# Where an attention stage turns its keys and queries: other slots, and the evictions shared out anew

## The chip, the cores and the metric

The kernel runs on one core of one Trainium2 chip. The metric is the device time of one execution in microseconds; of a kernel with several runs the median is given. The profile is that of one execution.

## The reference, cut to what matters

The program is a two-layer encoder trunk over 1024 tokens of width 1024, in float32. Layer 0 mixes RWKV-7 and gated DeltaNet heads; layer 1 is softmax attention over chunks of 64 tokens, each against its own and the previous 8 chunks. Every layer then has an MLP and a gated embedding. The change lies in layer 1:

```python
def chunk_band_attention(h, w_qkv, q_g, k_g, rel_bias):
    qkv = (h @ w_qkv).reshape(bsz, seq, 3, C_HEADS, C_HEAD_DIM)
    q = rmsnorm(qkv[:, :, 0], q_g) * (C_HEAD_DIM ** -0.5)
    k = rmsnorm(qkv[:, :, 1], k_g)
    v = qkv[:, :, 2]
    ...
    s = jnp.einsum('bqhd,bkhd->bhqk', q_c, k_b).astype(jnp.float32) + bias
    s = jnp.where(valid, s, -jnp.inf)
    prob = jax.nn.softmax(s, -1).astype(v.dtype)
    return jnp.einsum('bhqk,bkhd->bqhd', prob, v_b)
```

and in what is begun beside it: the embedding's projection `rmsnorm(p[i] @ ple_w_proj[i], ple_norm_g[i])` and the output projection of the attention.

## The kernel before, in words

Every float32 operand of a matrix product is kept as a high part (rounded to the matmul's fp32r) and a low part (what the rounding left). ScalarE makes the high part, VectorE the low part by subtraction, and a product is three matmuls (high x high, high x low, low x high).

`attention` runs 73 steps, `k` from -8 to 64. The heads go in pairs; a pair has two tiles of 512 tokens, so there are 16 tiles `s`, each with four steps (two heads `h`, two blocks of 256 queries `blk`): step `k` belongs to tile `k // 4`. All of it is written in program order and kept so: `Pinned` (L105) wraps VectorE, ScalarE and GpSimd, and `mm` and `tr` do the same for TensorE. Each engine works through its list in order, so an instruction that waits holds up all behind it on its engine.

A step is woven from these pieces, with `fill()` between them, which gives TensorE the next three matmuls of the projections (`dense`, eight times in a step):

- `evict(k+7)`: a projected block goes from its bank (`dps`) to `qk` and `vs` (two ScalarE activations, one VectorE subtraction). In some steps a weight is loaded (L1906) and split (`wq`).
- `values(k-1)` (probabilities times values, to `po`) and, every second step, `outs` (`otmp` on ScalarE, `y` on VectorE).
- first slot: `scores(k+1, 0)`, `turn(k, 0)`, `exps(k+1, 0)`, `low(k, 0)`.
- second slot: `scores(k+1, 1)`, `turn(k, 1)`, `turn(k, 2)`, `exps(k+1, 1)`, `low(k, 1)`, `low(k, 2)`.

`scores` writes the only scores buffer (`sc`, two PSUM banks). VectorE reads it at once in one instruction that adds the bias and takes the row's minimum (`pb,mx<-sc,toep`, a second small instruction fetches `mx`). The next `scores` can't begin before that. `exps` is the exponential on ScalarE, `turn` transposes 128 x 128 blocks of probabilities on TensorE into a bank `pt` and copies the high part out (`ptile`), `low` makes the low part on VectorE. `pt` banks come from a pool of three, taken in turn (`bank`, L1980). A step needs two or three of them, by the number of key blocks. Steps of an even tile's second block need two, of an odd tile's three.

Before the scores of tile `s`, its queries and keys must be normalised and turned:

- `squares` (GpSimd) and `sums` (VectorE) in steps 4s-5 and 4s-4, then `norms(s)` in step 4s-4: 14 small GpSimd instructions on 16 columns (`ss`, `nn`, `rsw`) and two products of 512 columns (`qk<-qk,nn`), keys first.
- `heads(s, 1)` at the end of step 4s-3 (`k % 4 == 1`): four transposes of the keys into a bank, then the evictions to `F1`, `k` of the tile. Per head one ScalarE activation (high part, 64 x 512, scaled by `kg`) and one VectorE operation (low part into the other half of the partitions).
- `heads(s, 0)` in step 4s-2, after `outs` and ahead of that step's first scores: four transposes of the queries, per head a ScalarE activation to `F0` and a VectorE operation to `Ql`, alternating, then two more ScalarE activations that write the high part a second time, into the other half of the partitions.

The projections' stream (`filler`, L2249 of before) goes on after the last `dense` with the embedding's projection `ple`. `ple` squares its blocks on ScalarE, adds them up on GpSimd (`act<-act,sq`, L2198) and ends with `row_stats`: sixteen column sums on TensorE (`dps<-ones,act`) and a small chain on VectorE (L282 to L287, L375) for `prsc`, which is next read in the second half of the MLP. After it comes `out_first`, the output projection of the first half of the tokens, which waits for the attention's outputs.

Of the kernel before, what the change touches and what calls it, by code (L numbers as in the profile page):

```python
# [8 lines left out]
F32 = mybir.dt.float32  # L9
F32R = mybir.dt.float32r  # L10
I32 = mybir.dt.int32
AF = mybir.ActivationFunctionType
ALU = mybir.AluOpType
# [102 lines left out]
class Trunk:  # L116
# [1775 lines left out]
    def attention(self, l1):  # L1892


        nc, tc, a, psm, sm, wp = self.nc, self.tc, self.a, self.psm, self.sm, self.wp
        V, A, G = (Pinned(tc, e) for e in (nc.vector, nc.scalar, nc.gpsimd))
        self.pinned, self.done = True, {}
        W, raws, toeps, dps, ST, JOB = {0: self.wq}, {}, {}, {}, {}, {}
        halves = (slice(0, 64), slice(64, 128))
# [62 lines left out]
        def norms(s):  # L1962
            st = ST[s]
            ss = st["ss"]
            nn = sm.tile([P, 16], F32, tag="nn1", name="nn1")
            w = sm.tile([P, 16], F32, tag="rswq", name="rsw")
            G.tensor_scalar(ss, ss, 1.0 / 64, 1e-6, op0=ALU.mult, op1=ALU.add)
            G.tensor_scalar(nn.bitcast(I32), ss.bitcast(I32), -0.5, 1597463007.0, op0=ALU.mult, op1=ALU.add)
            for _ in range(3):
                G.tensor_tensor(w, nn, nn, op=ALU.mult)  # L1970
                G.tensor_tensor(w, w, ss, op=ALU.mult)
                G.tensor_scalar(w, w, -0.5, 1.5, op0=ALU.mult, op1=ALU.add)
                G.tensor_tensor(nn, nn, w, op=ALU.mult)
            q5 = st["qk"].rearrange("p i (j h d) -> p i j h d", j=2, h=2)
            n4 = nn.rearrange("p (i j h) -> p i j h", i=4, j=2)
            for j in (1, 0):
                n = n4[:, :, j, :].rearrange("p i (h o) -> p i h o", o=1).broadcast_to((P, 4, 2, 64))
                G.tensor_tensor(q5[:, :, j], q5[:, :, j], n, op=ALU.mult)

        def bank():  # L1980
            return psm.tile([P, HB], F32, tag="pt", name="pt", bufs=3)

        def heads(s, j):
            st, qk = ST[s], ST[s]["qk"]
            g = self.vec("kg") if j else self.dv["qg8"]
            pt = bank()
            for e in range(4):
                self.tr(pt[:, e * P:(e + 1) * P], qk[:, e, j * P:(j + 1) * P], self.ident)
            if j:
                F = st["k"] = l1.tile([P, 2, HB], F32R, tag="F1", name="F1", bufs=3)  # L1990
            else:
                F = st["Q"] = self.xp.tile([P, 2, HB], F32R, tag=f"x{6 + s % 2}", name="F0")
                lo = st["Ql"] = self.ql[s % 2]
                if s < 2:
                    for h in range(2):
                        G.memset(lo[h][64 * (1 - h):64 * (2 - h)].bitcast(F32), 0.0)
            for h in range(2):
                r, o = halves[h], halves[1 - h]
                A.activation(F[r, h], pt[r], AF.Copy, scale=g[r])
                V.scalar_tensor_tensor(F[o, h] if j else lo[h][r], pt[r], g[r], F[r, h].bitcast(F32),  # L2000
                                       op0=ALU.mult, op1=ALU.subtract)
            if not j:
                for h in range(2):
                    r, o = halves[h], halves[1 - h]
                    A.activation(F[o, h], pt[r], AF.Copy, scale=g[r])

        def job(k):
            if k in JOB:
# [66 lines left out]
        def low(k, b):  # L2075
            jb = JOB[k]
            if b < len(jb["used"]):
                t, pt, u = jb["pts"][b]
                V.tensor_tensor(t[:, 1, u], pt[:, u], t[:, 0, u].bitcast(F32), op=ALU.subtract)
# [43 lines left out]
        E = {}  # L2123
# [45 lines left out]
        def y_split(q, hf):  # L2169
            t, raw = self.act([P, 2, 2, HB], F32R), yraw.pop((q, hf))  # L2170
            for e in range(2):
                ys[2 * q + e, hf] = t[:, e]
                if (q, e, hf) == (3, 1, 1):
                    self.ylast = t[:, e]
                else:
                    self.split_scaled(t[:, e], raw[:, e], None, slice(0, HB))

        def ple():
            act = self.act
            acc = act([P, 2, HB], F32, "b")  # L2180
            t = [act([P, 2, 2, HB], F32) for _ in range(4)]
            self.pnd = [self.dr.tile([P, 2, HB], F32, tag=f"pnd{k}", name="pnd") for k in range(NK)]
            self.prsc = self.cst.tile([P, NT], F32, tag="prsc", name="prsc")
            for n in range(NK):
                if n % 4 == 0:
                    hi, lo = late(n // 4)
                for hf in range(2):
                    ps = self.bank()
                    hs = slice(hf * HB, hf * HB + HB)
                    for k in range(2):  # L2190
                        o = slice(256 * (n % 4) + P * k, 256 * (n % 4) + P * k + P)
                        self.mm3(ps, hi[:, o], lo[:, o], E["w"][k][:, 0, hs], E["w"][k][:, 1, hs], k == 0, k == 1)
                        yield 0
                    nc.vector.tensor_scalar(t[n // 2][:, n % 2, hf, :], ps, self.dv["hpleg"][:, 8 + n:9 + n], None, op0=ALU.mult)
                    sq = acc[:, hf, :] if n == 0 else wp.tile([P, HB], F32, tag="sq", name="sq", bufs=1)
                    nc.scalar.activation(sq, ps, AF.Square)
                    if n:
                        nc.gpsimd.tensor_tensor(acc[:, hf, :], acc[:, hf, :], sq, op=ALU.add)  # L2198
                nc.sync.dma_start(out=self.pnd[n], in_=t[n // 2][:, n % 2])
            self.row_stats([acc[:, 0, :], acc[:, 1, :]], self.prsc)  # L2200

        def out_first():
            self.xh = [self.dr.tile([P, HB], F32, tag=f"xh{k}", name="xh") for k in range(NK)]
            self.order, self.wod = list(range(8)), {}
            yield ("ys", 0)
            y, x4 = {k: ys[k, 0] for k in range(8)}, None
            for n in range(NK):
                w = late(2 + n)
                if n > 1:
                    self.wod[n] = self.dr.tile([P, 2, T], F32, tag=f"wod{n}", name="wod")  # L2210
                    for e in range(2):
                        nc.sync.dma_start(out=self.wod[n][:, e], in_=w[e].bitcast(F32))
                if n % 4 == 0:
                    x4 = self.act([P, 4, HB], F32)
                x = x4[:, n % 4, :]
                nc.sync.dma_start(out=x, in_=self.xd[n][:, 0:HB])

                def ev(ps):
                    nc.vector.tensor_tensor(x, x, ps, op=ALU.add)
                    nc.sync.dma_start(out=self.xh[n], in_=x)  # L2220
                if n == 4:
                    y_load(0, 1)
                if n == 5:
                    y_split(0, 1)
                    y_load(1, 1)
                if n == 6:
                    y_split(1, 1)
                    y_load(2, 1)
                yield from self.dense_part(w, y, ev, self.order)
            y_split(2, 1)  # L2230
            y_load(3, 1)
            ws = [late(10), late(11)]
            self.first = [self.bank() for _ in ws]

            def part(ks):
                for (hi, lo), ps in zip(ws, self.first):
                    for k in ks:
                        o = slice(k * P, k * P + P)
                        self.mm3(ps, hi[:, o], lo[:, o], ys[k, 1][:, 0, :], ys[k, 1][:, 1, :], k == 0, k == 7)
                        yield 0  # L2240
            yield from part(range(6))
            y_split(3, 1)
            self.done["ylast", 0] = 0
            yield from part([6])
            yield ("at", 15)
            yield from part([7])
            self.y = {k: ys[k, 1] for k in range(8)}
# [19 lines left out]
        has = lambda k: 0 <= k < 64  # L2267
        for k in range(-8, 65):
# [37 lines left out]
            if has(k - 1) and k % 2 == 0:  # L2306
                outs(k - 1)
                if k % 4 == 0:
                    finish(k // 4 - 1)
            if k % 4 == 2 and has(k + 2):  # L2310
                heads((k + 2) // 4, 0)
            if has(k + 5) and k % 4 == 3:
                squares((k + 5) // 4, 0)
            if has(k + 4) and k % 4 == 0:
# [8 lines left out]
            fill()  # L2323
            if has(k):
                low(k, 0)
            if has(k + 1):
                scores(k + 1, 1)
            if has(k + 5) and k % 4 == 3:
                sums((k + 5) // 4, 0)
            if has(k + 4) and k % 4 == 0:  # L2330
# [11 lines left out]
                low(k, 1)  # L2342
                low(k, 2)
            if k % 4 == 1 and has(k + 3):
                heads((k + 3) // 4, 1)
            fill()
            if k == -8:
                ps = bank()
# [101 lines left out]
```

## Time and profile before

| | us |
|---|---|
| median of 3 runs | 3072.59 (3068.97 to 3077.63) |
| the profiled execution | 3075.75 |
| its span | 3074.0 |
| TensorE busy (share of the span) | 2947.6 (96%) |
| mean granted TensorE clock | 0.976 of full speed |
| attention stage, from the first `evict` to the last `values` | about 1686 to 2265 |

A row of the timeline gives start, duration, engine, source line, operation, output<-inputs, shape and count, and in brackets how long the engine had stood idle before and what ended that. Two instructions of one kind that follow each other are merged into one row. A row of the waits gives the total, the number of times and the longest. A row of the windows gives the stretch, its length, the busy time and count of PE, PEld, DVE, ACT and POOL, the granted clock, the DMA share and GB/s. PE is TensorE, PEld its weight load, DVE VectorE, ACT ScalarE, POOL GpSimd. L113 is the line of the wrapper, so names of tiles tell such rows apart: `F` is `F0` or `F1`.

### The profile page before, as it was taken

How to read it: one execution, taken by the hardware profiler on the slowest of the kernel's cores; microseconds unless marked ns; L12 is line 12 of the kernel's file. 1: busy time of each engine (PE TensorE's matmuls, PEld its weight loads, DVE VectorE, ACT ScalarE, POOL GpSimd, SP SyncE). 2: the span in 40 equal slices, each digit the busy share in tenths (PEclk: the TensorE clock that was granted, in tenths of full speed). 3: DMA queues.
4: the chain of work that ended last, by engine and by line, in shares of the span. 5: the costliest groups of instructions: out<-in, count | busy, mean ns of one | idle time of the engine just before them, and what ended most of it. 6: DMA issues, size and time to landing. Idle time of an engine off the chain costs nothing. (4 is left out here: it accounts for less than half of the span.)

```text
span 3074.0 us, 45073 instructions
## 1 busy us (share of the span) xinstructions
PE 2947.6 (96%) x16792; PEld 2472.8 (80%) x16792; DVE 2112.4 (69%) x3248; ACT 1412.6 (46%) x2546; POOL 1355.1 (44%) x1668
## 2 busy tenths in 40 slices
PE   8999999999989999999999999999899999999999
PEld 6888778887777888788887888888687888788887
DVE  6756765667758788877676456566647888877672
ACT  4444443444435444543333465566635444543331
POOL 5535533445504766554534322222403666645442
PEclk9999989999999999999999999999999999999999
DMA  3231212212544433754324111111355444654322
GB/s 129 95 96 56 76 42 77 75 59 88 174 169 155 156 149 151 263 182 157 124 89 136 43 38 47 40 40 59 129 203 189 154 151 151 223 209 177 124 96 101
DMA packets 166764, 374.30 MB, mean 122 GB/s; under 512 B 41360, under 2 KB 45584, under 8 KB 165136
## 3 DMA queue, kind: packets, MB, share of 16 engines
q1 hardware_dynamic: 134288, 312.68, 29.5%
q10 hardware_dynamic: 32256, 58.73, 5.0%
q8 instruction: 132, 2.16, 0.3%
q14 instruction: 88, 0.72, 0.1%
HBM read 259.15 MB, written 112.20 MB: 121 GB/s over the span
## 5 line engine op out<-in xcount | busy, mean ns | idle before, releaser
L173 PE MATMUL dps<-r,act 128*128 128x512 f32 x4440 | 1045.2, 394 | 13.1 <-DVE act L113 8.5
L173 PEld LDWEIGHTS dps<-r,act 128*128 128x128 f32 x4440 | 836.5, 189 | 204.6 <-DVE act L113 15.2
L173 PE MATMUL dps<-xg,whi 128*128 128x512 f32 x1248 | 419.7, 414 | 14.1 <-ACT xg L343 6.9
L113 ACT CAST act<-late 128x512 fp32r<-128x512 f32 (+1 forms) x282 | 205.5, 731 | 442.9 <-DVE late L113 258.1
L113 DVE TENSOR_TENSOR act<-late,act 128x512 fp32r<-128x512 f32 (+1 forms) x282 | 330.0, 1172 | 71.5 <-ACT act L113 68.2
L173 PE MATMUL dps<-wq,act 128*128 128x384 f32 x1536 | 340.9, 353 | 1.1 <-ACT gw L1738 0.9
L173 PEld LDWEIGHTS dps<-xg,whi 128*128 128x128 f32 x1248 | 236.3, 195 | 64.8 <-ACT xg L343 6.8
L173 PEld LDWEIGHTS dps<-wq,act 128*128 128x128 f32 x1536 | 264.4, 193 | 4.8 <-ACT gw L1738 1.3
L173 PE MATMUL dps<-xg,wlo 128*128 128x512 f32 x624 | 256.3, 411 | 0.0
L113 POOL TENSOR_TENSOR late<-late 128x512 f32<-128x512 f32 (+1 forms) x104 | 187.8, 1813 | 81.4 <-ACT late L113 58.4
L113 POOL TENSOR_TENSOR late<-late,rs 128x512 f32<-128x512 f32 x88 | 137.5, 1575 | 101.5 <-DVE late L113 94.0
L113 DVE TENSOR_TENSOR r<-act,r 128x1024 fp32r<-128x1024 f32 (+1 forms) x80 | 139.2, 1741 | 6.7 <-ACT r L113 6.7
L113 DVE TENSOR_TENSOR late<-late 128x512 f32<-128x512 f32 x120 | 142.3, 1186 | 1.0
L173 PEld LDWEIGHTS dps<-xg,wlo 128*128 128x128 f32 x624 | 121.2, 194 | 25.7 <-DVE wlo L300 0.4
L173 PE MATMUL dps<-xw,act 128*128 128x512 f32 x576 | 137.8, 392 | 0.0
L113 ACT CAST ptile<-pt 128x512 fp32r<-128x512 f32 (+1 forms) x144 | 74.0, 515 | 134.7 <-PE pt L178 134.3
L113 DVE TENSOR_TENSOR ptile<-pt,ptile 128x512 fp32r<-128x512 f32 (+1 forms) x144 | 83.9, 600 | 68.2 <-ACT ptile L113 67.2
L173 PEld LDWEIGHTS dps<-xw,act 128*128 128x128 f32 x576 | 108.4, 188 | 24.2
L300 DVE TENSOR_TENSOR wlo<-wraw,whi 128x1024 fp32r<-128x1024 f32 x76 | 95.1, 1253 | 39.2 <-ACT whi L299 38.3
L299 ACT CAST whi<-wraw 128x1024 fp32r<-128x1024 f32 x76 | 79.6, 1048 | 89.2 <-PE dps L173 45.9
L113 DVE TENSOR_TENSOR late<-late,dps 128x512 f32<-128x512 f32 x154 | 104.6, 682 | 19.7 <-ACT late L113 15.9
L113 ACT ACTIVATE late<-late 128x512 f32<-128x512 f32 x176 | 110.6, 631 | 13.5 <-POOL late L113 9.8
(509 smaller groups left out, 5711.2 us busy)
## 6 DMA issues: line engine op xcount, KB each, us to landing
late<-in_w SPq DMA_DIRECT2D x100, 512.0 KB
hc<-late ACTq DMA_DIRECT2D x154, 256.0 KB
act<-hc SPq DMA_DIRECT2D x76, 512.0 KB
wraw<-in_w_in SPq DMA_DIRECT2D x56, 512.0 KB
hraw<-hc SPq DMA_DIRECT2D x36, 512.0 KB
hc<-sums ACTq DMA_DIRECT2D x70, 256.0 KB
act<-in_w SPq DMA_DIRECT2D x28, 512.0 KB
wraw<-in_w_out SPq DMA_DIRECT2D x21, 512.0 KB
```

The costliest lines, as they stand in the source:

```text
L113: return lambda *args, **kw: self.tc.keep_in_program_order(f(*args, **kw))
L173: r = self.nc.tensor.matmul(out, lhsT, rhs, start=start, stop=stop)
L299: nc.scalar.copy(hi, raw)
L300: nc.vector.tensor_tensor(lo, raw, hi.bitcast(F32), op=ALU.subtract)
```

## The change

It has five parts. (1) `heads` no longer alternates: both ScalarE high parts come first, then both VectorE low parts, the latter in a function that is returned and called later. (2) For queries, the second copy of the high part is made by GpSimd from the first, where ScalarE read it from the bank again. (3) Keys are turned in the second slot of step 4s-3: the transposes and high parts ahead of that slot's scores, the low parts behind them. Queries are turned at the end of the same step, half a step earlier than before. (4) `norms` runs on VectorE for tile 0, where nothing else is there to be done yet. (5) `ple` no longer ends with `row_stats`; it is called after the second block of `out_first`.

```diff
@@ norms
+            G = V if s == 0 else Pinned(tc, nc.gpsimd)
@@ heads
             for h in range(2):
                 r, o = halves[h], halves[1 - h]
                 A.activation(F[r, h], pt[r], AF.Copy, scale=g[r])
-                V.scalar_tensor_tensor(F[o, h] if j else lo[h][r], pt[r], g[r], F[r, h].bitcast(F32),
-                                       op0=ALU.mult, op1=ALU.subtract)
-            if not j:
+
+            def low():
                 for h in range(2):
                     r, o = halves[h], halves[1 - h]
-                    A.activation(F[o, h], pt[r], AF.Copy, scale=g[r])
+                    V.scalar_tensor_tensor(F[o, h] if j else lo[h][r], pt[r], g[r], F[r, h].bitcast(F32),
+                                           op0=ALU.mult, op1=ALU.subtract)
+                if not j:
+                    for h in range(2):
+                        G.tensor_copy(F[halves[1 - h], h], F[halves[h], h])
+            return low
@@ ple
-            self.row_stats([acc[:, 0, :], acc[:, 1, :]], self.prsc)
+            E["acc"] = [acc[:, 0, :], acc[:, 1, :]]
@@ out_first
                 yield from self.dense_part(w, y, ev, self.order)
+                if n == 1:
+                    self.row_stats(E["acc"], self.prsc)
@@ attention, the steps
-            if k % 4 == 2 and has(k + 2):
-                heads((k + 2) // 4, 0)
...
+            key = k % 4 == 1 and has(k + 3) and heads((k + 3) // 4, 1)
             if has(k + 1):
                 scores(k + 1, 1)
+            if key:
+                key()
...
             if k % 4 == 1 and has(k + 3):
-                heads((k + 3) // 4, 1)
+                heads((k + 3) // 4, 0)()
```

On TensorE, in the step that turns the keys of tile 4 (`pt<-ident,qk` are the transposes of keys or queries, `pt<-ident,pb` those of probabilities, `sc` the scores, `dps<-wq` the projection), this stood before, from the second slot's last scores to the step's end:

```order
L173 MATMUL sc<-F_16667,Ql 128x256
L173 MATMUL dps<-wq_16041,act 128x384
L173 MATMUL dps<-wq_16042,act 128x384
L173 MATMUL dps<-wq_16041,act 128x384
L178 MATMUL pt<-ident,pb 128x128 x4
L173 MATMUL dps<-wq_16041,act 128x384
L173 MATMUL dps<-wq_16042,act 128x384
L173 MATMUL dps<-wq_16041,act 128x384
L178 MATMUL pt<-ident,pb 128x128 x2
L178 MATMUL pt<-ident,qk 128x128 x4
```

The changed kernel has, from just before that slot's scores:

```order
L178 MATMUL pt<-ident,qk 128x128 x4
L173 MATMUL sc<-F_16283,F_16677 128x384
L173 MATMUL sc<-F_16283,Ql 128x384
L173 MATMUL sc<-F_16647,F_16677 128x256
L173 MATMUL sc<-F_16647,Ql 128x256
L173 MATMUL dps<-wq_16041,act 128x384
L173 MATMUL dps<-wq_16042,act 128x384
L173 MATMUL dps<-wq_16041,act 128x384
```

and, behind these, to the step's end:

```order
L178 MATMUL pt<-ident,pb 128x128 x4
L173 MATMUL dps<-wq_16041,act 128x384
L173 MATMUL dps<-wq_16042,act 128x384
L173 MATMUL dps<-wq_16041,act 128x384
L178 MATMUL pt<-ident,pb 128x128 x2
L178 MATMUL pt<-ident,qk 128x128 x4
```

The first `qk` row is now the keys, ahead of the scores; the last, where the keys stood, is the queries.

On VectorE, at the same place, this stood before, from the second slot's reading of the scores (`ISA pb,mx<-sc,toep`) to the first one of the next step (`F` low parts of the keys, `Ql` those of the queries):

```order
L113 ISA pb,mx<-sc,toep 128x640
L113 ISA mx 128x1
L113 TENSOR_TENSOR ptile<-pt,ptile 128x512
L113 TENSOR_TENSOR ptile<-pt,ptile 128x256
L113 SCALAR_TENSOR_TENSOR F_17028<-pt,vecs,F_17028 64x512 x2
L113 SCALAR_TENSOR_TENSOR vs<-dps,rscol,vs 128x128
L113 TENSOR_TENSOR y<-po,otmp 64x512
L113 SCALAR_TENSOR_TENSOR Ql<-pt,d_qg_85,F_17070 64x512 x2
L113 ISA pb,mx<-sc,toep 128x640
```

and this stands there now:

```order
L113 ISA pb,mx<-sc,toep 128x640
L113 ISA mx 128x1
L113 SCALAR_TENSOR_TENSOR F_16999<-pt,vecs,F_16999 64x512 x2
L113 TENSOR_TENSOR ptile<-pt,ptile 128x512
L113 TENSOR_TENSOR ptile<-pt,ptile 128x256
L113 SCALAR_TENSOR_TENSOR Ql<-pt,d_qg_85,F_17038 64x512 x2
L113 SCALAR_TENSOR_TENSOR vs<-dps,rscol,vs 128x128
L113 TENSOR_TENSOR y<-po,otmp 64x512
L113 ISA pb,mx<-sc,toep 128x640
```

The keys' low parts moved ahead of the probabilities' low parts, the queries' ahead of `vs` and `y`.

## The prediction

> **What bounds the kernel now.** I read the shares of the engines first, then TensorE's own waits inside the attention stage (1690 to 2265 us), then the timeline of single steps. TensorE has by far the most to do:
>
> ```profile
> PE 2947.6 (96%) x16792; PEld 2472.8 (80%) x16792; DVE 2112.4 (69%) x3248; ACT 1412.6 (46%) x2546; POOL 1355.1 (44%) x1668
> ```
>
> So a stall of TensorE is time, and what another engine gains is none unless TensorE waited for it. In the attention stage its two largest waits are these (total, times, longest):
>
> ```profile
> PE sc L173 <- DVE mx L113: 43.0, 25, 3.5
> PE dps L173 <- POOL act L2198: 4.2, 1, 4.2
> ```
>
> The first row is a scores matmul that waits until VectorE has read the one scores buffer (`mx` ends that reading). The timeline shows where. Here is a step pair after which a tile with an odd number is turned (tile 3); its step has two probability banks, and I call it short:
>
> ```profile
> 1796.97 0.28 PE L173 MATMUL sc<-F,F 128*128 128x256 f32 x1
> ...
> 1797.37 2.06 POOL L113 TENSOR_TENSOR qk<-qk,nn 128x512 f32<-128x512 f32 x2
> ...
> 1798.32 0.48 ACT L113 CAST ptile<-pt 128x384 fp32r<-128x384 f32 x1 [0.65 <-PE pt L178]
> 1798.59 0.60 PE L178 MATMUL pt<-ident,qk 128*128 128x128 f32 x4
> 1798.71 0.51 ACT L113 ACTIVATE pb<-pb,mx 128x256 f32<-128x256 f32 x1
> ...
> 1802.23 0.35 DVE L113 SCALAR_TENSOR_TENSOR vs<-dps,rscol,vs 128x128 fp32r<-128x128 f32 x1
> 1802.44 0.42 PE L173 MATMUL sc<-F,F 128*128 128x384 f32 x1
> ...
> 1802.80 0.68 DVE L113 TENSOR_TENSOR y<-po,otmp 64x512 f32<-64x512 f32 x1 [0.22 <-ACT otmp L113]
> ...
> 1804.29 0.68 ACT L113 ACTIVATE F<-pt,d_qg 64x512 fp32r<-64x512 f32 x1 [0.81 <-DVE Ql L113]
> 1805.01 0.76 DVE L113 SCALAR_TENSOR_TENSOR Ql<-pt,d_qg,F 64x512 fp32r<-64x512 f32 x1 [0.75 <-ACT F L113]
> 1805.79 0.56 DVE L113 CUSTOM_DVE_ANT_0 pb<-sc,toep 128x384 f32<-128x384 f32 x1
> ...
> 1806.42 0.50 PE L173 MATMUL sc<-F,F 128*128 128x512 f32 x1 [2.01 <-DVE mx L113]
> ```
>
> The scores of 1802.44 are not read until 1805.79, because the query evictions (Ql, in a chain ACT, DVE, ACT, DVE) stand in front of that reading. TensorE stops 2.01 us. Even tiles (three banks, long) lose 2.19, and the last three tiles 3.04, 2.20 and 3.46:
>
> ```profile
> 1828.69 2.06 POOL L113 TENSOR_TENSOR qk<-qk,nn 128x512 f32<-128x512 f32 x2
> ...
> 1829.35 0.34 PE L173 MATMUL sc<-F,F 128*128 128x384 f32 x1
> ...
> 1831.65 0.60 PE L178 MATMUL pt<-ident,qk 128*128 128x128 f32 x4
> ...
> 1832.00 1.81 PE L173 MATMUL dps<-wq,act 128*128 128x384 f32 x9
> ...
> 1840.44 0.47 PE L173 MATMUL sc<-F,F 128*128 128x128 f32 x1 [2.19 <-DVE mx L113]
> ...
> 2132.74 0.50 PE L173 MATMUL sc<-F,F 128*128 128x512 f32 x1 [3.04 <-DVE mx L113]
> 2167.78 0.37 PE L173 MATMUL sc<-F,F 128*128 128x128 f32 x1 [2.20 <-DVE mx L113]
> ...
> 2211.49 0.50 PE L173 MATMUL sc<-F,F 128*128 128x512 f32 x1 [3.46 <-DVE mx L113]
> ```
>
> **The change, part by part.**
>
> *Queries at the step's end.* They leave the place in front of the reading, 15 times: tiles 1 to 12 at 6 x 2.01 + 6 x 2.19 = 25.2, with the last three 33.9 us. What is late next there? In a short step I follow the two queues from the new order. ScalarE: the key's two high parts, the cast of 0.48, the exponential of 0.51 with its sum (0.70 together), the query's two high parts. The evictions last:
>
> ```profile
> L113 ACT ACTIVATE F<-pt,vecs x32: 668/682/686, 1709.3 to 2205.0; 64x512 fp32r<-64x512 f32 x32
> L113 DVE SCALAR_TENSOR_TENSOR Ql<-pt,d_qg,F x32: 733/750/758, 1712.8 to 2210.1; 64x512 fp32r<-64x512 f32 x32
> ```
>
> With the key transposes ending at 1799.08 (below) that gives 1800.55, 1801.05, 1801.6 and 1803.0; VectorE adds two query low parts of 0.75 (1804.55), vs 0.35 and y 0.68, and starts the reading at 1805.6, done after 0.6 at 1806.2. TensorE, later by the key wait, wants the buffer at 1805.9. A stall of 0.3 stays, 7 x 0.3 = 2.1. In a long step the same walk ends the reading at 1839.2, TensorE comes at 1839.7: none.
>
> *Keys in the second slot.* The transposes now stand ahead of the slot's scores, so at 1796.97 and 1829.35, and must wait for GpSimd's multiplication of the keys (the first half of the qk rows): 1797.37 + 1.05 = 1798.42 and 1828.69 + 1.05 = 1829.74. That is a new stall of 1.5 in the 7 short steps, 10.5 us, and 0.45 in six of the 7 long ones, 2.7 (at tile 14 the keys were ready in time). GpSimd's chain begins a step earlier, behind VectorE's sums, where the change moves nothing, so it ends when it did. For tile 15 GpSimd is later still:
>
> ```profile
> 2196.74 0.31 PE L173 MATMUL sc<-F,F 128*128 128x256 f32 x1
> ...
> 2200.00 2.07 POOL L113 TENSOR_TENSOR qk<-qk,nn 128x512 f32<-128x512 f32 x2
> ...
> 2201.12 0.66 PE L178 MATMUL pt<-ident,qk 128*128 128x128 f32 x4 [1.44 <-POOL qk L113]
> ```
>
> 4.3 us in place of the 1.44 there and about 0.5 between: 2.4 more. Behind the waiting transposes everything of TensorE is queued, for it runs in order.
>
> *The banks.* Three banks `pt` go round. In a long step the new order fills all three before the queries, whose transposes need the key's bank. Its last reader is VectorE's second key low part: transposes end 1829.80 + 0.60 = 1830.40, two high parts end 1831.88, two low parts 1833.45. TensorE comes to the query transposes at 1831.65 + 0.45 + 0.35 (one set of four, 1831.65 to 1832.00) = 1832.45 and waits 1.0: 7 x 1.0 = 7 us. In short steps the bank is free.
>
> *GpSimd's copies* replace two ScalarE evictions. Nearest rows for their price:
>
> ```profile
> L113 POOL COPY rl<-l x16: 609/610/1098, 1748.1 to 2257.5; 128x512 f32<-128x512 f32 x16
> ```
>
> ```profile
> 1826.71 1.23 DVE L113 TENSOR_TENSOR wq<-wraw,wq 128x1024 fp32r<-128x1024 f32 x1 [0.58 <-ACT wq L113]
> ...
> 1826.93 1.09 POOL L113 TENSOR_TENSOR rsw<-rsw,ss 128x16 f32<-128x16 f32 x1
> ```
>
> 0.6 to 1.1 each, so ready some 2 us after the query's high parts; the first scores that need them come a step and a half, some 12 us, later: nothing, for that step covers them. Were it gone, the scores would wait up to 2.2. The last two rows show a GpSimd operation on 16 columns that takes as long as VectorE's weight split beside it. [...] In these steps no weight split stands behind the copies, so I take 0 for VectorE too.
>
> *Tile 0.* VectorE takes over its normalisation, and tile 0's queries go too:
>
> ```profile
> 1701.53 0.69 DVE L113 TENSOR_REDUCE ss<-sq 128x8 f32<-128x512 f32 x1 [0.77 <-POOL sq L113]
> ...
> 1708.59 0.66 PE L178 MATMUL pt<-ident,qk 128*128 128x128 f32 x4 [1.17 <-POOL qk L113]
> ...
> 1719.69 0.39 PE L173 MATMUL sc<-F,F 128*128 128x256 f32 x1 [2.32 <-DVE mx L113]
> ```
>
> ```profile
> L285 DVE TENSOR_TENSOR rsw<-prsc 128x8 f32<-128x8 f32 x3 | 0.5, 167 | 0.1
> ```
>
> The last row is VectorE's nearest to the fourteen small operations; with a little between them I take 0.2 each. From 1702.2 they end at 1705, and a product of 0.7 (y above) to 1.05 (GpSimd's) gives keys at about 1706, when the transposes are due: 1.1 gained. The 2.32 falls to about half (the scores' reading still waits for a weight split): 1.1. Together 2.2; between 0 and 3.5.
>
> *Row sums.* They move behind two blocks of the output projection:
>
> ```profile
> 2229.30 3.84 PE L173 MATMUL dps<-ones,act 128*128 128x1 f32 x16 [4.23 <-POOL act L2198]
> ...
> 2234.75 1.05 ACT L2153 CAST wq<-wraw 128x1024 fp32r<-128x1024 f32 x1 [4.88 <-DMA wraw<-in_w_out]
> ```
>
> The 4.23 goes, for the sums of GpSimd are long done by then; but the second row is next on that path, and its weights land when they land. I take 4.2, between 0 and 6.
>
> *The clock.* After some of the stalls TensorE ran at half clock (the granted clock is the third number from the end):
>
> ```profile
> 1840.00:1844.00 4.00, 3.56 (x13) 3.27 (x14) 1.81 (x5) 2.49 (x6) 0.00 (x0) 0.57 0.00 0
> 2132.00:2136.00 4.00, 3.26 (x12) 3.19 (x13) 2.43 (x6) 3.46 (x6) 0.00 (x0) 0.73 0.07 20
> 2168.00:2172.00 4.00, 4.00 (x17) 3.68 (x17) 1.58 (x4) 2.37 (x5) 0.00 (x0) 0.58 0.00 0
> ```
>
> The first and the last lose (1 - 0.575) x 4 = 1.7 us each; I take that for all three. They follow the stalls of 2.19, 3.04 and 2.20. The new stalls are at most 1.5 (but for tile 15), so I let all three go: 5.1 us, between 0 and 5.1. [...]
>
> *Sum*: -33.9 + 2.1 + 10.5 + 2.7 + 2.4 + 7.0 = -9.2; -2.2, -4.2, -5.1: **-20.7 us**. The profiled execution took 3075.75 (span 3074.0 and 1.75 around it), which gives 3055.0; it lies 3.2 above the median of 3072.6, so I predict 3072.6 - 20.7 = **3052**.
>
> **Rivals.**
> A, *only the attention counts*: the clock stays as it is, the row sums' 4.2 returns as the wait for weights, and the short steps keep 0.8, not 0.3: -9.2 - 2.2 + 3.5 = -7.9, 3065. For it: the wait of 4.88; against it: the clock's rows. 0.18.
> B, *slower*: the queries' evictions reach VectorE so late that the reading of the scores still waits for them. It has 1.7 us of room in the short step (1804.55 against some 1806.2); ScalarE's queue there is full from 1799.2 on, and one more wait of that size decides. Then the old stalls stay and the new ones come on top: +15.6 + 7.0 - 2.2 - 4.2 = +16, 3089. Against it: the evictions no longer alternate (0.81 and 0.75 of idling fall away). 0.09.
> C, *the copies hold VectorE up*: as GpSimd's 1.09 waits out VectorE's split, VectorE could wait out two copies of 0.6 in all 15 tiles, 15 x 1.2 = 18, leaving -3, 3070. Against it: the rows show it only the one way round. 0.03. [...]
> The forecast has 0.70.
>
> **How the numbers follow.** A change within 0.3% (9.2 us) can't be told from none. Faster by more: the forecast and a little of A, 0.72; A and C mostly inside, 0.19; slower 0.09. The range: without bank wait and short-step remainder (9 us) and with 2 us more at the row sums 3041; with rival C and without part of the tail 3072. B is left out.
>
> **What would show it.** Right: the 2.01 and 2.19 behind `mx` are gone, TensorE waits for `qk` of GpSimd some 1.5 us at odd tiles, 0.45 at even ones, 4 at the last; the query transposes wait about 1 for VectorE at even tiles; no 4.23 at the row sums; half clock only in the last tiles. Wrong: stalls of 2 us behind `mx` in these steps (B), key waits well over 1.5, or a scores row that waits for GpSimd's copies.

## The result, and the profile after

The changed kernel took 3051.94 us (median of 4 runs) beside 3070.78 us before; the ratio is 0.9932 (0.9909 to 0.9955). The prediction was 3052 from 3072.6. A second set of runs gave 3058.57 us beside 3076.9, ratio 0.9935 (0.9916 to 0.9953).

One of the first four executions, the profiled one, ran at a granted TensorE clock of 0.55 throughout (4754 us); it is in the median of 3051.94 but not in the ratio, and the other three have a median of 3049.85. The rows of "after" below are from the second set's profile, at 0.974. Its engines:

```profile
span 3059.7 us, 45090 instructions
## 1 busy us (share of the span) xinstructions
PE 2946.8 (96%) x16792; PEld 2469.6 (81%) x16792; DVE 2120.9 (69%) x3264; ACT 1393.2 (46%) x2514; POOL 1369.1 (45%) x1684
```

TensorE does the same work as before. Its four largest waits from 1680 to 2300 us (total, times, longest):

```profile
PE pt L178 <- POOL qk L113: 15.5, 14, 4.1
PE pt L178 <- DVE F L113: 6.3, 7, 1.2
PE sc L173 <- DVE mx L113: 6.3, 7, 2.3
PE po L173 <- ACT ptile L113: 3.9, 1, 3.9
```

The 43.0 us behind the reading of the scores (`mx`) have become 6.3. Two waits stand in their place: the key transposes wait for GpSimd's `qk`, the query transposes of even tiles for VectorE's low parts of the keys, `F`. This is the step pair of tile 3 in the timeline, whose rows of before stand in the prediction:

```profile
1800.19 2.06 POOL L113 TENSOR_TENSOR qk<-qk,nn 128x512 f32<-128x512 f32 x2
...
1801.29 0.66 PE L178 MATMUL pt<-ident,qk 128*128 128x128 f32 x4 [1.38 <-POOL qk L113]
...
1801.98 1.38 ACT L113 ACTIVATE F<-pt,vecs 64x512 fp32r<-64x512 f32 x2 [1.53 <-PE pt L178]
...
1803.40 1.51 DVE L113 SCALAR_TENSOR_TENSOR F<-pt,vecs,F 64x512 fp32r<-64x512 f32 x2 [0.74 <-ACT F L113]
...
1804.40 1.38 ACT L113 ACTIVATE F<-pt,d_qg 64x512 fp32r<-64x512 f32 x2
...
1805.20 1.28 POOL L113 CAST F<-F 64x512 fp32r<-64x512 f32 x2 [2.96 <-ACT F L113]
...
1805.81 1.51 DVE L113 SCALAR_TENSOR_TENSOR Ql<-pt,d_qg,F 64x512 fp32r<-64x512 f32 x2 [0.31 <-ACT F L113]
...
1807.62 0.67 DVE L113 TENSOR_TENSOR y<-po,otmp 64x512 f32<-64x512 f32 x1
...
1808.22 0.54 DVE L113 CUSTOM_DVE_ANT_0 pb<-sc,toep 128x384 f32<-128x384 f32 x1
...
1808.83 0.50 PE L173 MATMUL sc<-F,F 128*128 128x512 f32 x1
```

The keys make TensorE wait 1.38 us. The query evictions end before `vs` and `y`, and the scores of 1808.83 have no bracket: no wait is left where there were 2.01. GpSimd's two copies take 1.28 us together and hold nobody. In a long step (tile 4), at tile 13, at the last tile, and where the row sums were, the timeline has:

```profile
1835.20 0.63 PE L178 MATMUL pt<-ident,qk 128*128 128x128 f32 x4 [0.85 <-DVE F L113]
...
2123.30 0.50 PE L173 MATMUL sc<-F,F 128*128 128x512 f32 x1 [1.28 <-DVE mx L113]
...
2187.82 1.11 PE L178 MATMUL pt<-ident,qk 128*128 128x128 f32 x4 [4.13 <-POOL qk L113]
...
2200.60 0.50 PE L173 MATMUL sc<-F,F 128*128 128x512 f32 x1 [1.27 <-DVE mx L113]
...
2218.78 0.33 PE L173 MATMUL sc<-F,F 128*128 128x128 f32 x1 [2.32 <-DVE mx L113]
...
2223.13 1.04 ACT L2158 CAST wq<-wraw 128x1024 fp32r<-128x1024 f32 x1 [3.44 <-DMA wraw<-in_w_out]
...
2224.71 0.58 PE L173 MATMUL po<-ptile,vs 128*128 128x256 f32 x1 [3.85 <-ACT ptile L113]
```

To measure the attention by itself, I cut every trace at the same three places of TensorE's list: the ends of its matmuls 10,001, 12,595 and 13,994 of 16,792. The first piece is the attention up to tile 13, the second the last tiles, the embedding's projection, and the output projection up to the start of the MLP; the row sums lie in the second in all kernels. The windows of the first profile of before, and of the changed kernel:

```profile
1670.12:2112.47 442.35, 405.68 (x2597) 386.76 (x2596) 256.23 (x525) 252.93 (x546) 118.31 (x285) 0.98 0.14 48
2112.47:2419.63 307.16, 280.96 (x1400) 237.10 (x1400) 204.29 (x322) 158.46 (x297) 101.02 (x121) 0.96 0.44 157
```

```profile
1681.71:2103.22 421.51, 401.24 (x2597) 382.19 (x2596) 259.31 (x541) 236.51 (x520) 128.26 (x294) 0.99 0.15 51
2103.22:2404.20 300.98, 276.90 (x1401) 232.65 (x1400) 203.47 (x321) 154.75 (x290) 104.40 (x127) 0.97 0.45 160
```

I call the two lengths together the stretch: 749.5 us before, 722.5 now, 27.0 less. By the windows, 18.5 of these are idle time of TensorE that is gone (62.9 us before, 44.3 now), and 8.5 are shorter busy time: in the stretch TensorE spent 41.0 us at half clock before and 23.9 now. Behind the stretch the two kernels take 654.4 and 655.5 us. The changed kernel starts the stretch 11.6 us later (1681.71 against 1670.12); that is work which the change does not touch, and the first experiment asks why.

### The profile page after: what moved, and what is told of

Read it like the earlier page. It is cut to its first block, busy times and chain, and to the rows that moved or that the text cites. A ratio compares the mean times of both kernels' runs of the same rounds, so it can differ in the third digit from the quotient of the medians.

```text
span 4752.7 us, 45090 instructions
## 1 busy us (share of the span) xinstructions
PE 4721.4 (99%) x16792; PEld 3064.8 (64%) x16792; DVE 2068.5 (44%) x3264; ACT 1400.3 (29%) x2514; POOL 1352.0 (28%) x1684
## 4 chain that ended last, share of the span: by engine, by line
PE 98%; DVE 1%; DMA 0%; ACT 0%; issue 0%; POOL 0%; SPq 0%; ACTq 0%; DVEq 0%
PE dps L173 80%; PE pt L178 3%; PE po L173 3%; PE ch L173 3%; PE sc L173 2%; PE iz L173 2%; PE pm L173 2%; PE tp L173 1%; PE py L173 1%; PE tp L178 0%; PE pp L178 0%; PE pm L178 0%; PE st L173 0%; PE pp L173 0%; PE iz L178 0%; PE dps L178 0%
## 5 line engine op out<-in xcount | busy, mean ns | idle before, releaser
L173 PE MATMUL dps<-r,act 128*128 128x512 f32 x4440 | 1725.5, 577 | 0.0
L173 PEld LDWEIGHTS dps<-r,act 128*128 128x128 f32 x4440 | 972.5, 219 | 732.6 <-issue 429.6
L173 PE MATMUL dps<-xg,whi 128*128 128x512 f32 x1248 | 625.8, 593 | 12.3 <-ACT xg L343 6.9
L173 PE MATMUL dps<-wq,act 128*128 128x384 f32 x1536 | 520.8, 492 | 0.0
L173 PEld LDWEIGHTS dps<-xg,whi 128*128 128x128 f32 x1248 | 286.0, 235 | 174.9 <-issue 86.7
L173 PEld LDWEIGHTS dps<-wq,act 128*128 128x128 f32 x1536 | 332.4, 229 | 73.7 <-issue 4.8
L173 PE MATMUL dps<-xg,wlo 128*128 128x512 f32 x624 | 368.6, 591 | 0.0
L113 DVE TENSOR_TENSOR act<-late,act 128x512 fp32r<-128x512 f32 (+1 forms) x282 | 269.1, 962 | 40.3 <-ACT act L113 40.2
L173 PE MATMUL dps<-xw,act 128*128 128x512 f32 x576 | 227.8, 576 | 0.0
L173 PE MATMUL dps<-act 128*128 128x512 f32 x384 | 154.2, 577 | 0.0
```

The lines of the kernel that those rows point to most:

```text
L113: return lambda *args, **kw: self.tc.keep_in_program_order(f(*args, **kw))
L173: r = self.nc.tensor.matmul(out, lhsT, rhs, start=start, stop=stop)
```

## The experiments

All times of kernels stand beside runs of the kernel before on the same chip; the stretch is read from each profile.

**before_again**: the kernel before, unchanged.

> The kernel before, once more, for a second profile. The stretch ahead of the attention stage, whose code the change leaves alone, ended at 1624 us in the first profile of before and at 1627 to 1636 in four profiles of the changed kernel and its variants. Theory (that stretch varies from run to run): its end falls anywhere between 1620 and 1640, while the attention stage itself repeats within 1 us and has the 43 us of waits for the reading of the scores. Rival (the change slows the stretch ahead of it): it ends again at 1624.

Its windows:

```profile
1675.90:2115.91 440.01, 403.23 (x2596) 384.44 (x2596) 256.25 (x525) 253.15 (x546) 118.60 (x285) 0.99 0.15 49
2115.91:2421.99 306.08, 280.30 (x1400) 235.04 (x1400) 203.59 (x322) 158.55 (x297) 101.10 (x121) 0.97 0.45 158
```

The stretch began at 1675.9, not 1670.1, and took 746.1 us, with the same stalls. In twelve profiles of before and of kernels that share its start it began between 1669 and 1683, and the kernels that began earliest and latest were both variants of the changed one. So the code ahead varies by 14 us from run to run, and that variation is in every total; that the change slows it is not borne out. The theory allowed 1 us between the two stretches and they differ by 3.4, of which 3.1 are busy time of TensorE; the second profile spent 10.2 us less at half clock (last section). Each kernel below has one profile, so a difference of this size between two stretches settles nothing by itself; there the single waits decide.

**changed_again**: the profile shown above.

> The changed kernel as it is, for a profile at the full clock. Theory (the prediction): about 20 us under the kernel before; in the attention stage TensorE no longer waits 2.0 to 2.2 us for VectorE's reading of the scores, waits about 1.5 us for GpSimd's keys at the odd tiles, 0.45 at the even ones and 4 at the last, and about 1.0 for a bank at the query transposes of even tiles; nothing at the row sums. Rival (the sum came out right by accident): the key waits or the bank waits are missing or twice as long, and another term makes up for it.

Key waits of 1.37 to 1.40 at the seven odd tiles, 0.3 at six even ones and 4.13 at the last; bank waits of 0.85, six times, and 1.20. "Nothing at the row sums" was wrong: TensorE waits 3.85 us for `ptile` there.

**rowsums_back**

```diff
-            E["acc"] = [acc[:, 0, :], acc[:, 1, :]]
+            self.row_stats([acc[:, 0, :], acc[:, 1, :]], self.prsc)
...
-                if n == 1:
-                    self.row_stats(E["acc"], self.prsc)
```

> Only the row sums go back to the end of the embedding's projection. Theory: TensorE waits again some 4.2 us for GpSimd's sum there, and the kernel takes 4 us more than the changed one (0 to 6). Rival: the weights of the output projection land when they land, the wait for them gets shorter by what the row sums take, and the time is the changed kernel's within 1 us.

3051.77 us, ratio 0.9918 (0.9902 to 0.9934). The profiled execution is 9.6 us faster than that of the changed kernel, but 8.1 of these lie ahead of the stretch. TensorE's wait came back, and with it another went, in the timeline of this kernel:

```profile
2209.20 3.83 PE L173 MATMUL dps<-ones,act 128*128 128x1 f32 x16 [4.23 <-POOL act L2203]
...
2213.46 1.04 ACT L2158 CAST wq<-wraw 128x1024 fp32r<-128x1024 f32 x1 [3.68 <-DMA wraw<-in_w_out]
```

There is the 4.23, but no 3.85 for `ptile`, and the 2.32 for the scores is 1.41. The stretch takes 722.3 us against 722.5: the rival holds, the move of the row sums gained nothing. In both kernels ScalarE stands at the same cast of a weight block until its load has landed. In the changed kernel the probabilities' cast (`ptile`) is queued behind it and TensorE has nothing else to do; with the row sums in place TensorE spends that time on them.

**norm0_back**

```diff
-            G = V if s == 0 else Pinned(tc, nc.gpsimd)
```

> Only tile 0's normalisation goes back to GpSimd. Theory: the first key transposes wait 1 us or more for GpSimd again (they now stand half a step earlier, so up to 3), and the kernel takes 1 to 3 us more than the changed one. Rival: something else (the first weight splits, the first reading of the scores) holds TensorE at the same place, and it takes under 0.5 us more.

3060.26 us, ratio 0.9937 (0.9916 to 0.9958): the totals can't tell. The stretch takes 727.0 us, 4.5 more than the changed kernel's; its first piece alone takes 426.2, 4.7 more. In the timeline and in one window of this kernel:

```profile
1714.61 0.66 PE L178 MATMUL pt<-ident,qk 128*128 128x128 f32 x4 [2.22 <-POOL qk L113]
```

```profile
1715.80:1719.10 3.30, 3.30 (x13) 3.20 (x13) 1.60 (x3) 2.34 (x5) 1.54 (x4) 0.50 0.01 2
```

The wait of 2.22 came back, and behind it the 3.30 us of that window ran at half clock (0.50), some 1.7 us of lost work; the changed kernel had 1.00 there. The theory's wait is right; its price missed the clock. The remaining 0.8 us I did not trace.

**scalar_copies**

```diff
+            if not j:
+                for h in range(2):
+                    r, o = halves[h], halves[1 - h]
+                    A.activation(F[o, h], pt[r], AF.Copy, scale=g[r])
...
-                if not j:
-                    for h in range(2):
-                        G.tensor_copy(F[halves[1 - h], h], F[halves[h], h])
```

> Only the queries' second high part is made by ScalarE from the bank again (after both high parts, ahead of VectorE's low parts in the order); GpSimd copies nothing. Theory (GpSimd's copies save ScalarE time that is not on the path): the bank is held 1.4 us longer and the exponential and vs evictions of the next step come 1.4 us later; with 96% of TensorE busy this costs 0 to 0.5 us a tile, 0 to 7 us in all, taken as 2. [...]

3065.92 us, ratio 0.9969 (0.9956 to 0.9981): most of the gain is lost; the stretch takes 734.5 us, 12.0 more, of which 11.1 are idle time of TensorE; it spent 10.2 us less at half clock. The theory missed: it allowed 7 us at the most. The short step of tile 3 in this kernel's timeline:

```profile
1808.20 2.76 ACT L113 ACTIVATE F<-pt,d_qg 64x512 fp32r<-64x512 f32 x4
...
1810.99 1.51 DVE L113 SCALAR_TENSOR_TENSOR Ql<-pt,d_qg,F 64x512 fp32r<-64x512 f32 x2 [1.69 <-ACT F L113]
...
1814.00 0.51 PE L173 MATMUL sc<-F,F 128*128 128x512 f32 x1 [1.43 <-DVE mx L113]
```

VectorE's first low part waits until ScalarE is done with all four readings of the bank, 1.38 us later than with two; then `vs`, `y` and the reading of the scores come as much later. TensorE stalls about 1.43 us at the odd tiles 1 to 11, 2.65 at tile 13, and 0.56 at even ones. ScalarE's time in this place is on the path, and against this order the copies' move to GpSimd is worth about 12 us. ScalarE copies behind the low parts, as the kernel before had them, were not tried in the new slot.

**alternating_queries**

```diff
             for h in range(2):
                 r, o = halves[h], halves[1 - h]
                 A.activation(F[r, h], pt[r], AF.Copy, scale=g[r])
+                if not j:
+                    V.scalar_tensor_tensor(lo[h][r], pt[r], g[r], F[r, h].bitcast(F32),
+                                           op0=ALU.mult, op1=ALU.subtract)
...
             def low():
...
+                if j:
```

> The changed kernel, but the queries' evictions alternate again (high part, low part, high part, low part); GpSimd keeps the copies. In the changed kernel's trace VectorE's first low part starts only when both high parts are done, so both orders take the same 2 x 0.68 + 2 x 0.75 us in a row. Theory A (what counts is when ScalarE is free again, as in scalar_copies): ScalarE is done 0.8 us later, so its vs, qk and otmp evictions, then y, then the reading of the scores come 0.8 later: 0.8 us at the 7 odd tiles and the last, nothing at the even ones, which had room: 5 to 7 us slower than the changed kernel. Theory B (the low parts are the end of the chain): no difference, within 1 us in the attention stage.

3056.08 us, ratio 0.9938 (0.9917 to 0.9958); the stretch takes 729.2 us, 6.7 more, of which 4.8 are idle time of TensorE (it also spent 6.8 us more at half clock). It has stalls of 0.70 to 0.72 behind the reading at the odd tiles 1 to 11, 0.5 more at tile 13, 1.0 more at the last, and none of that kind at the even ones:

```profile
1795.76 0.68 ACT L113 ACTIVATE F<-pt,d_qg 64x512 fp32r<-64x512 f32 x1 [1.12 <-DVE Ql L113]
...
1797.22 0.58 ACT L113 COPY otmp<-po 64x512 f32<-64x512 f32 x1
...
1797.83 0.68 DVE L113 TENSOR_TENSOR y<-po,otmp 64x512 f32<-64x512 f32 x1 [0.22 <-ACT otmp L113]
...
1799.04 0.50 PE L173 MATMUL sc<-F,F 128*128 128x512 f32 x1 [0.70 <-DVE mx L113]
```

Theory A holds. In size, the waits for the reading rise from 6.3 to 12.1 us, 5.8 where it said 5 to 7; in way, ScalarE's second reading of the bank waits 1.12 us for VectorE's first low part, so ScalarE comes to `otmp` later, `y` waits for it, and the reading of the scores stands behind `y`.

**keys_end**

```diff
-            key = k % 4 == 1 and has(k + 3) and heads((k + 3) // 4, 1)
...
-            if key:
-                key()
...
             if k % 4 == 1 and has(k + 3):
+                heads((k + 3) // 4, 1)()
                 heads((k + 3) // 4, 0)()
```

> Keys are turned at the end of the step, straight ahead of the queries, both with high parts first. By the walk of the prediction: the keys are ready, so the 15.5 us of waits for GpSimd and the 6.3 for the bank go; but VectorE's two low parts of the keys now follow the probabilities' and stand between them and the next reading of the scores: 0.5 to 1 us in the 7 short steps, less in the long ones, 5 to 10 us. Then it is 10 to 15 us faster than the changed kernel, and turning the keys earlier bought nothing. Rival (the second slot is needed): the reading of the scores is held up by about 2 us in all 15 tiles, 30 us, and it is 5 to 10 us slower than the changed kernel.

3046.91 us, ratio 0.9907 (0.9892 to 0.9923); the stretch takes 709.8 us, 12.7 less than the changed kernel's. Its waits from 1665 to 2300 us:

```profile
PE sc L173 <- DVE mx L113: 10.6, 20, 2.3
PE pt L178 <- POOL qk L113: 3.7, 8, 1.4
...
PE pt L178 <- DVE ptile L113: 2.6, 7, 0.4
```

The first theory holds: most of the 15.5 us for GpSimd and all of the 6.3 for the key's bank are gone (2.6 behind `ptile` are new), the waits for the reading grew only from 6.3 to 10.6, and turning the keys in the second slot, as the change does it, costs about 13 us.

**early_norms**

```diff
+            if has(k + 4) and k % 4 == 0:
+                squares((k + 4) // 4, 1)
+                sums((k + 4) // 4, 1)
+                norms((k + 4) // 4)
             if has(k - 1) and k % 2 == 0:
                 outs(k - 1)
...
-            if has(k + 4) and k % 4 == 0:
-                squares((k + 4) // 4, 1)
...
-            if has(k + 4) and k % 4 == 0:
-                sums((k + 4) // 4, 1)
-                norms((k + 4) // 4)
```

> The changed kernel, but the second squares, the sums and the normalisation of a tile stand ahead of the outputs of their step, half a step earlier. In the changed kernel's trace the second squares end at 1791.0, VectorE idles from 1790.3 to 1791.9, and the sums run only at 1795.25. Theory (the keys wait for GpSimd because VectorE's sums stand late in its list): the chain begins 3.5 us earlier, the 1.4 us at odd tiles and the 0.3 at even ones go, most of the 4.1 at the last too, some 12 to 15 us, less 0.5 us a tile at the most for sums that VectorE does ahead of the outputs: 8 to 15 us faster than the changed kernel. Rival (GpSimd itself is late, held by other work): the keys wait as long as before and the time is the changed kernel's.

3037.49 us, ratio 0.9878 (0.9860 to 0.9896); the stretch takes 705.8 us, 16.7 less than the changed kernel's. Its two largest waits from 1680 to 2300 us:

```profile
PE pt L178 <- DVE F L113: 8.4, 7, 1.2
PE sc L173 <- DVE mx L113: 7.5, 7, 2.3
```

No row with GpSimd's `qk` is left, and the theory holds, a little beyond its 8 to 15 us. The keys had waited because VectorE did their sums some 4 us later than it could: for tile 3 the second squares start at 1789.96 us in the changed kernel and at 1790.02 here, the sums behind them at 1795.25 and at 1791.10. The bank wait grew from 0.85 to 1.20.

**early_norms_keys_end**: early_norms and the edit of keys_end together.

> As early_norms, but keys and queries are turned one after the other at the end of the step, as in keys_end. Theory (once the keys are ready in time, it matters little in which slot they are turned): the waits for GpSimd of keys_end go (7 x 0.32 and the 1.4 of the last tile, 3.7 us), those for VectorE stay (7 x 0.37 for the bank, about 7 x 0.4 and 7 x 0.26 for the reading): 2 to 5 us faster than keys_end in the attention stage, within 3 us of early_norms. Rival (the second slot is worth something when the keys are ready): 5 us or more slower than early_norms.

3043.73 us, ratio 0.9888 (0.9870 to 0.9906); the stretch takes 711.6 us. The theory fails and the rival holds: it is 1.8 us slower than keys_end (with 5.7 us more idle time of TensorE) and 5.8 slower than early_norms. The 3.7 us for GpSimd are gone, but the waits for the reading of the scores grow from 10.6 to 19.7 us (21 waits): TensorE is at that reading sooner, VectorE is not. With the keys ready the second slot is worth about 6 us; by the order of VectorE's list that is because it takes the keys' low parts out of the queue in front of the reading.

**early_norms_late_queries**

```diff
-            if k % 4 == 1 and has(k + 3):
-                heads((k + 3) // 4, 0)()
             fill()
+            if k % 4 == 1 and has(k + 3):
+                heads((k + 3) // 4, 0)()
```

> As early_norms, and besides the step's last three matmuls of the projection go ahead of the queries' transposes. Theory (the query transposes of even tiles wait 0.85 us for VectorE to be done with the key's bank): three matmuls take 0.75 us, so 7 x 0.75, some 5 us more than early_norms gains, as long as the reading of the scores, which comes up to 0.75 us later, was not yet what TensorE waits for. Rival (it was): the same time appears as waits for that reading, and the two kernels take the same time.

3034.58 us, ratio 0.9867 (0.9854 to 0.9880), the lowest of all; the stretch takes 703.9 us. The bank wait falls from 1.20 to 0.68, 7 x 0.52 = 3.6 us, less than three matmuls' 0.75, and part of that returns: 9.1 us in 13 waits for the reading, where early_norms had 7.5 in 7. The stretch is 1.9 us shorter than that of early_norms, between the theory's 5 and the rival's nothing. Against early_norms the medians differ by 2.9 us with overlapping intervals, so the order of these two is not settled; both beat the changed kernel.

**queries_next_step**

```diff
             fill()
+            if k % 4 == 2 and has(k + 2):
+                heads((k + 2) // 4, 0)()
             if has(k + 7):
                 evict(k + 7)
```

> As early_norms_late_queries, but the queries' transposes stand another three matmuls later, behind the first ones of the next step and ahead of that step's evictions. Theory (the 0.68 us at even tiles is still the bank): the 0.68 goes, 7 x 0.68 = 4.8 us, and the reading of the scores comes 0.75 us later at all tiles, which costs nothing at even tiles and up to 0.75 at the 7 odd ones: between 5 us faster and 1 us slower than early_norms_late_queries. Rival (the reading is again what TensorE waits for): waits for it of 0.5 us or more in all 15 tiles, 3 to 8 us slower.

3043.95 us, ratio 0.9892 (0.9870 to 0.9913); the stretch takes 708.9 us, 5.0 more than early_norms_late_queries, 2.3 of it idle time of TensorE, the rest busy time, with 6.8 us more at half clock. The bank wait is down to 0.16, and the reading costs 0.74 to 0.76 at the odd tiles 1 to 11 and 0.22 to 0.25 at even ones. What the bank gives (4.8 us to 1.0) the reading takes (9.1 to 14.2). The theory's range is missed. The rival's 3 to 8 us is met, and the reading is again what TensorE waits for, but the 0.5 us that it named for all tiles shows at odd ones only.

## Why the prediction was right

The total came out at 3052, and so did the mechanism; some terms were off and cancelled. Each against its measurement:

| step of the prediction | forecast | measured |
|---|---|---|
| query stalls of before go | -33.9 | -33.9, none of these stalls is left whole |
| remainder at the reading | +2.1, in 7 short steps | +2.6: 1.28 at tile 13 and 1.27 at tile 15, none elsewhere |
| key waits, odd tiles | +10.5 | +9.6 |
| key waits, even tiles | +2.7 | +1.7 (six of about 0.3) |
| key wait, last tile | +2.4 (4.3 for 1.44 and 0.5) | +2.7 (4.13 for 1.44) |
| bank | +7.0 | +6.3 |
| tile 0 | -2.2 | -4.8: the waits of 1.17 and 2.32 became one of 0.40, and 1.7 of clock |
| second readings of odd tiles' next steps | none | -3.3 |
| row sums | -4.2 | 0 |
| clock | -5.1 | -8.5 and -3.4 against the two profiles of before, tile 0's 1.7 in it |

Together, with tile 0's clock counted once, the terms make -25.9 against the first profile of before and -20.8 against the second; the stretch shortened by 27.0 and 23.6.

*Queries and keys.* The walk through the queues held to a few tenths at tiles 1 to 12. In the short step it put the reading at 1805.6 with the second slot at 1796.97; in the trace that slot was due at 1801.29 - 1.38 = 1799.91, 2.94 later, and the reading began at 1808.22 against 1805.6 + 2.94 = 1808.54. That is why no remainder of 0.3 is seen. At tile 13, where 3.04 fell to 1.28, the prediction put the same 0.3 without following that step, and at the last tile, where 3.46 fell to 1.27, nothing. The queries' move was not taken back alone in any run; that it removed the old stalls rests on the two traces and on alternating_queries, which keeps the new slot and has 0.70 us where before had 2.01. Nor did the prediction see that the old stalls echoed: one step further on, before waited 0.55 us for the reading at six odd tiles,

```profile
1813.46 0.45 PE L173 MATMUL sc<-F,F 128*128 128x384 f32 x1 [0.55 <-DVE mx L113]
```

and the changed kernel doesn't:

```profile
1815.17 0.34 PE L173 MATMUL sc<-F,F 128*128 128x384 f32 x1
```

*Row sums* are the step that failed: "The 4.23 goes". It went, and the next thing on that path was the weight load, which the prediction named as rival A's. 4.2 us of gain was not there.

*Tile 0* was mis-sized: the 2.32 fell to 0.40 where the prediction let half of it stay, and it did not count the half clock behind the old stall there (1720, 1.7 us).

*Clock.* That the half clock of 1840, 2132 and 2168 goes was right. But 1840 was no fixed cost of before: the second profile does not have it. The term also went by the length of a stall alone, though two stalls of 2.19 us in one profile were followed by different clocks (last section), and it left out the half clock behind the stalls at 1720, 2212 and 2240, 3.41 us each.

*Rivals.* B did not happen, but it was nearer than 0.09 of chance and "1.7 us of room" said. That room was a misreading of the prediction's own walk: it set the end of the queries' low parts (1804.55) against the end of the reading (some 1806.2), though `vs`, `y` and the reading still lie between, and the same walk ended the reading 0.3 us after TensorE's 1805.9. In the trace of the short step the reading ended at 1808.22 + 0.54 = 1808.76, and TensorE began at 1808.83: almost no room was left, and 1.38 us more of ScalarE (scalar_copies) or a return to alternation brought stalls of 1.43 and 0.70. C is refuted: VectorE's low parts take 750 ns at the median in both kernels, and the copies' move gained 12 us (against scalar_copies) instead of losing 18.

*The sum.* The medians differ by 18.8 (20.9 with the three executions at full clock) and 18.3 us, the ratios make 20 to 21, the stretch 27.0 and 23.6. The code ahead of the stretch varies by 14 us from run to run, more than these differ; the agreement of the total to a tenth of a microsecond is chance.

## What to carry to other kernels

Where one buffer's reader is late, follow each engine's list in order from the new place and price every instruction that now stands ahead of that reader; here that gave the stalls of tiles 1 to 12 to a few tenths, and the runs showed that an instruction moved earlier (the keys) is worth something only when its input is moved earlier too. A wait that disappears is worth its length only if nothing else, such as a load with its own landing time, ends at the same point. Where the untouched part of a kernel varies by more than the effect, compare the same stretch of instructions in the traces, not the totals.

## What the runs showed of the hardware

In the first profile of before, two stalls of 2.19 us (ending at 1775.66 and 1840.44) were followed by different clocks. The windows are 3.41 us long, which is how long the half clock lasted behind the second one, and lie whole multiples of that apart. So do the starts of all seven stretches of half clock in that profile between 1700 and 2340 us. For each stall there are two neighbouring windows:

```profile
1772.00:1775.42 3.42, 1.47 (x10) 1.12 (x9) 2.61 (x4) 1.78 (x3) 0.00 (x0) 1.00 0.00 0
1775.42:1778.83 3.41, 3.17 (x20) 3.01 (x21) 2.16 (x6) 3.19 (x8) 0.00 (x0) 1.00 0.00 0
1836.85:1840.27 3.42, 1.40 (x10) 1.04 (x8) 2.61 (x4) 1.77 (x4) 0.00 (x0) 1.00 0.01 2
1840.27:1843.68 3.41, 3.24 (x12) 2.95 (x12) 1.54 (x5) 2.17 (x4) 0.00 (x0) 0.50 0.00 0
```

With 3.41 - 1.47 = 1.94 us idle the next window had the full clock, with 3.41 - 1.40 = 2.01 half. In the second profile of before the same stall as at 1840, 2.20 us there, was followed by the full clock:

```profile
1845.29 0.33 PE L173 MATMUL sc<-F,F 128*128 128x128 f32 x1 [2.20 <-DVE mx L113]
```

```profile
1845.30:1848.70 3.40, 3.40 (x22) 3.24 (x23) 2.21 (x5) 3.19 (x7) 0.00 (x0) 1.00 0.00 0
```

In the first profile, TensorE idled 2.01 to 3.32 us in the 3.41 us ahead of each of those seven stretches; in the other 173 such windows at full clock between 1700 and 2340 us it idled 1.94 us at the most, and full clock followed. Ahead of 1700 us the same profile has half clock behind 1.19 us of idling (1676.43 to 1679.84) and behind none (143.84 to 147.25); why is open. A stall of about 2 us thus cost 1.7 us more (3.41 us at a clock of 0.50) or nothing in these two profiles, which is part of the difference between them.

In the changed kernel GpSimd's copies of 64 x 512 took 0.61 us at the median of 32 (606 to 616 ns):

```profile
L113 POOL CAST F<-F x32: 606/610/616, 1719.0 to 2195.5; 64x512 fp32r<-64x512 f32 x32
```

ScalarE and VectorE did not read one bank at the same time in the rows above. In the changed kernel VectorE's first low part of the keys began at 1803.40, behind both of ScalarE's readings (1801.98 to 1803.36); in alternating_queries ScalarE's second reading waited 1.12 us for VectorE's first. Whether that comes from the chip or from the program's own synchronisation was not tried.
